# The gates of the latent attention from seven products of quarters

## The chip, the cores and the metric

One core of one Trainium2 chip runs the whole program. The metric is the device time of one execution in microseconds (us).

## The reference

The program is one layer of a diffusion backbone for 128 context tokens and 512 latent tokens, 1024 channels each. The normalised tokens `h` go through one wide input projection into four mixers (a recurrence and three attentions); each mixer's output is projected to 1024 channels, multiplied by a gate per token and channel, and the four are added:

```
h = rmsnorm(x) * (1 + sc1) + sh1
u = h @ w_in                       # among them the gates: 4 x 1024 channels
br[n] = o[n] @ w_branch[n]         # n: recurrence, window, latent, grouped attention
y = sum_n br[n] * sigmoid(gates[n]) @ w_out
```

After that come a norm, an MLP with squared ReLU (1024 to 4096 and back) and a second norm. The change concerns `sigmoid(gates[2])`, the gates of the latent attention: a product of the 1024 x 1024 columns of `w_in` with the 640 tokens.

## The kernel before

All 640 tokens (T) are worked on together. Operands of a product are kept as two parts, hi and lo, whose sum is the fp32 value; a product of a 128 x 128 weight block with 320 tokens (HALF) is three matmuls, hi x hi, hi x lo and lo x hi, added in PSUM (`t_steps`, L357, matmuls at L365 to L367). Weights come as fp32 tiles of 512 KB by DMA on SyncE's queue (`wload`, L311, tag `wr`), and `wsplit` (L322) makes hi by a copy (`copy_r`, L137 and L139, on GpSimd, or ScalarE where `wtile.act` is set, L329) and lo by a subtraction on VectorE (`rest`, L141 and L142). Each of the tags wr, wh and wl has three buffers (WBUFS).

`gates(n)` (L703) calls `gate_steps` (L692): for each of 8 blocks of 128 channels one weight tile, two token halves, for each half 8 blocks of the inner dimension and three matmuls into a bank `mm` (two of them), and a copy out by ScalarE (L698); after four blocks a sigmoid over the four (L701). `merge(n, ...)` (L971) projects a mixer's output in the same form, multiplies by the gates and adds to yT on VectorE (L984, L985).

The latent attention stands in `mla()` (L1037). It first projects the tokens to queries' and keys' latents (`tok_group`, 416 columns, banks of `sc_tile` and one `pv`), then, token tile by token tile (five of 128), squares and scales them (L1075 to L1082), rotates a part, makes `kr4` on GpSimd (L1059) and transposes the pieces on TensorE (L1052, L1061, L1095) into `cq` and `ckv`. Then follow `merge(3, ...)`, `sig = gates(n)`, the loads of w_uq and w_ukv (L1109), the queries' projection and the attention itself, beside which modulation weights (`wada`) go through the same `wr` buffers.

The order of instructions on each engine is fixed when the program is built: a planner takes, for each engine, what is ready by its own estimate of time, work that stands earlier in the program first. Around the change nothing else fixes an order. Buffers are shared by tags: `big` tiles of 2560 elements (14, SLOTS), `small` tiles (tag tk, four), P and PT of the attention units (two each, L760), banks `mm` and `sc` (two each; an sc tile is two banks, of which `sc_bank` uses one).

The MLP already uses the construction that the change brings to the gates: `token_sums` (L1358), `weight_sums` (L1372), `pair` (L1391) with `products` (L1315). There seven products of quarters (4 inner blocks, 320 tokens) stand for two channel blocks and two token halves.

Of the kernel before, what the change touches and what calls it, by code (L numbers as in the profile page):

```python
# [26 lines left out]
OFF = {}  # L27
# [37 lines left out]
def trunk(ctx, tc, I, O):  # L65
# [68 lines left out]
    def f(ap):  # L134
        return ap.bitcast(F32)
# [5 lines left out]
    def rest(out, src, hi):  # L141
        V.tensor_tensor(out=out, in0=src, in1=f(hi), op=ALU.subtract)  # L142
# [168 lines left out]
    def wload(rows, k0, c0, n, nk):  # L311

        raw = wp.tile([128, 1024], F32, tag="wr", name="wr")
        v = lambda t: t[:, 0:nk * n].rearrange("p (k n) -> p k n", k=nk)
        for part, src in rows(k0, nk, c0, n):
            dst = v(raw)[part]
            if len(src.shape) < 3 or len(dst.shape) < 3:
                dst = dst.rearrange("p (a d) -> p a d", d=src.shape[-1])
            dma(out=dst, in_=src)
        return raw  # L320
# [382 lines left out]
    def gates(n):  # L703
        sig = [big(F32, 4, T, name="sig") for _ in range(2)]
        for _ in gate_steps(n, sig):
            pass
        return sig
# [326 lines left out]
    sig3 = gates(3)  # L1034


    def mla():  # L1037
        n = 2
        MS = 96.0 ** -0.5
# [31 lines left out]
        for tt in range(NT):  # L1071
            ps = banks[tt]
            x = small(name="mtx")
            ssq = sm.tile([128, 2], F32, tag="ssq2", name="ssq2")
            S.activation(out=x[:, 0:256], in_=ps[:, 0:256], func=AF.Square, accum_out=ssq[:, 0:1])  # L1075
            S.activation(out=x[:, 256:384], in_=ps[:, 256:384], func=AF.Square, accum_out=ssq[:, 1:2])
            r = sm.tile([128, 2], F32, tag="rs2", name="rs2")
            V.tensor_scalar(out=ssq[:, 1:2], in0=ssq[:, 1:2], scalar1=2.0, scalar2=None, op0=ALU.mult)
            rsqrt_mean(ssq, 2, 256, r)
            V.scalar_tensor_tensor(out=x[:, 0:256], in0=ps[:, 0:256], scalar=r[:, 0:1], in1=qg, op0=ALU.mult, op1=ALU.mult)  # L1080
            V.scalar_tensor_tensor(out=x[:, 256:384], in0=ps[:, 256:384], scalar=r[:, 1:2], in1=kg, op0=ALU.mult, op1=ALU.mult)
            S.activation(out=x[:, 384:416], in_=ps[:, 384:416], func=AF.Copy)  # L1082
            if tt == 4:
                dma(out=O['mla_ckv'], in_=x[:, 256:384])
                dma(out=O['mla_kr'], in_=x[:, 384:416])
                kr = x[:, 384:416]
            else:
                kr = x[:, 416:448]
                rope(x[:, 384:416], 1, 32, tt, rope32, kr)
            key0 = 128 * (tt + 1)  # L1090
            ckv_T(x[:, 256:384], key0)
            kr_T(kr, key0)
            tp = tp_tile()
            for j in range(2):
                PE.transpose(out=tp[:, j], in_=x[:, 128 * j:128 * j + 128], identity=ident)  # L1095
            hi = cq[:, 0, :, 128 * tt:128 * tt + 128]
            S.activation(out=hi, in_=tp[:, 0:2], func=AF.Copy)
            rest(cq[:, 1, :, 128 * tt:128 * tt + 128], tp[:, 0:2], hi)
        merge(3, True, sig3)

        sig = gates(n)

        wu = {}
        for nm, src, nk, a, b in (('uq', I['mla_w_uq'][0], 2, 64, 32), ('ukv', I['mla_w_ukv'][0], 1, 64, 64)):
# [207 lines left out]
    def relu2_tile():  # L1312
        return mx.tile([128, HALF], F32, tag="relu2", name="relu2", bufs=3)

    def products(ps, w, x, start=True, stop=True):  # L1315
        for k in range(len(w)):
            PE.matmul(out=ps, lhsT=w[k][0], rhs=x[k][0], start=(start and k == 0), stop=False)  # L1317
            PE.matmul(out=ps, lhsT=w[k][0], rhs=x[k][1], start=False, stop=False)  # L1318
            PE.matmul(out=ps, lhsT=w[k][1], rhs=x[k][0], start=False, stop=(stop and k == len(w) - 1))  # L1319

    def block(w, m, th, parts=((0, HALF),)):

        ps, sq = mm_tile()[:, 0:HALF], relu2_tile()
# [45 lines left out]
            sums[i] = [(hi[:, k], lo[:, k]) for k in range(4)]  # L1369
        return [by_k(h2[0][0]), by_k(h2[1][0]), by_k(h2[1][1])] + [sums[i] for i in (1, 2, 3, 4)]  # L1370

    def weight_sums(c0):  # L1372

        r1, r2 = (wload(w1, 0, c0 + 128 * m, 128, 8) for m in range(2))
        sa = wp.tile([128, 1024], F32, tag="wr", name="ws")
        p, q = slice(0, 512), slice(512, 1024)

        def split(x, nk):
            hi, lo = wsplit(x, 128, nk)
            return [[(hi[:, k], lo[:, k]) for k in range(i, i + 4)] for i in range(0, nk, 4)]  # L1380
        a11, a12 = split(r1, 8)
        V.tensor_tensor(out=sa[:, q], in0=r2[:, p], in1=r2[:, q], op=ALU.add)
        V.tensor_tensor(out=sa[:, p], in0=sa[:, q], in1=r1[:, p], op=ALU.subtract)
        g2, g1 = split(sa, 8)
        V.tensor_tensor(out=r2[:, p], in0=r1[:, p], in1=r2[:, p], op=ALU.subtract)
        g3, a22 = split(r2, 8)
        V.tensor_tensor(out=r1[:, q], in0=r1[:, q], in1=sa[:, p], op=ALU.subtract)
        g4, = split(r1[:, q], 4)
        return a11, a12, a22, g1, g2, g3, g4

    def pair(c0, X, hid):  # L1391

        b11, b21, b22, t1, t2, t3, t4 = X
        a11, a12, a22, g1, g2, g3, g4 = weight_sums(c0)

        def product(w, x):
            ps = psl.tile([128, 512], F32, tag="pr", name="pr", bufs=5)[:, 0:HALF]
            products(ps, w, x)
            return ps
# [106 lines left out]
```

## Time and profile before

| | us |
|---|---|
| three runs | 1481.51, 1478.18, 1483.23 |
| median | 1481.51 |
| the profiled execution | 1480.22 |
| its span, first to last instruction | 1478.4 |
| TensorE busy | 1408.9 |
| VectorE busy | 908.0 |
| ScalarE busy | 521.6 |
| GpSimd busy | 396.2 |

PE is TensorE's matmul, PEld its weight load, DVE VectorE, ACT ScalarE, POOL GpSimd, SP SyncE (its queue issues the DMAs). Matmuls overlap, so their durations add up to more than they take; their starts tell the pace. Times of day in the trace are us from the start of the span.

### The profile page before, as it was taken

To read this page: it belongs to the slowest core of one execution; us is meant where nothing else is said; L and a number is where in the kernel's file an instruction comes from. 1 tells how busy PE (TensorE), PEld (TensorE's weight loads), DVE (VectorE), ACT (ScalarE), POOL (GpSimd) and SP (SyncE) were. 2 spreads that over 40 slices of the span, in tenths; PEclk is the share of its full clock that TensorE was granted. 3 is DMA by queue.
4 is the path that set the end of the run, shared out by engine and by line. 5 is a ranking of instruction groups with operands and counts; after the bars stand their busy time and mean duration, and the time that the engine had idled before them with its cause. 6 is when DMAs were issued, how large, how long until landed. Compare 5 with 4: busy or idle time off the path is not lost.

```text
span 1478.4 us, 26650 instructions
## 1 busy us (share of the span) xinstructions
PE 1408.9 (95%) x10825; PEld 1282.2 (87%) x10825; DVE 908.0 (61%) x1643; ACT 521.6 (35%) x1189; POOL 396.2 (27%) x430
## 2 busy tenths in 40 slices
PE   6999999999999899999998988998999999999996
PEld 5898998999899898999997677887988988988985
DVE  4347747466742697441824467656857758767865
ACT  4334343332544225442123565314532212321212
POOL 2015425233322445321313344123101001001014
PEclk9999999999999999999999999999999999999998
DMA  9421212122112131112223711232124332222321
GB/s 325 139 85 54 76 48 66 53 61 58 45 44 52 40 80 29 45 36 69 72 71 119 236 57 43 73 104 67 48 80 137 94 115 86 86 58 86 103 69 72
DMA packets 138227, 121.17 MB, mean 82 GB/s; under 512 B 22296, under 2 KB 119412, under 8 KB 138104
## 3 DMA queue, kind: packets, MB, share of 16 engines
q1 hardware_dynamic: 138104, 119.47, 27.4%
q8 instruction: 85, 1.39, 0.4%
q14 instruction: 38, 0.31, 0.1%
HBM read 115.96 MB, written 3.49 MB: 81 GB/s over the span
## 4 chain that ended last, share of the span: by engine, by line
PE 83%; DVE 8%; POOL 3%; ACT 3%; issue 3%; DMA 1%; DVEq 0%; POOLq 0%; ACTq 0%
PE mm L365 8%; PE mm L367 8%; PE mm L366 8%; PE out L381 5%; PE out L383 5%; PE out L382 5%; PE pr L1317 4%; PE pr L1318 4%; PE pr L1319 4%; PE tp L860 3%; PE pv L1013 3%; PE sc L383 3%; PE sc L381 3%; PE sc L382 2%; PE sc L953 2%
## 5 line engine op out<-in xcount | busy, mean ns | idle before, releaser
L142 DVE TENSOR_TENSOR wl<-wr,wh 128x1024 fp32r<-128x1024 f32 (+3 forms) x174 | 209.4, 1207 | 134.9 <-POOL wh L139 81.4
L139 POOL TENSOR_SCALAR wh<-wr 128x1024 fp32r<-128x1024 f32 (+2 forms) x108 | 121.0, 1122 | 549.9 <-PE pr L1319 246.6
L365 PE MATMUL mm<-hTh,wh 128*128 128x320 f32 x704 | 220.4, 313 | 2.0 <-DVE qA L520 0.9
L367 PE MATMUL mm<-hTh,wl 128*128 128x320 f32 x704 | 219.1, 311 | 0.0
L366 PE MATMUL mm<-hTl,wh 128*128 128x320 f32 x704 | 218.1, 310 | 0.0
L365 PEld LDWEIGHTS mm<-hTh,wh 128*128 128x128 f32 x704 | 132.2, 188 | 3.9 <-DVE qA L520 1.0
L813 POOL TENSOR_SCALAR P<-P,rden 128x640 f32<-128x640 f32 (+3 forms) x120 | 84.5, 713 | 183.4 <-DVE rden L825 87.3
L367 PEld LDWEIGHTS mm<-hTh,wl 128*128 128x128 f32 x704 | 132.2, 188 | 0.9 <-issue 0.7
L366 PEld LDWEIGHTS mm<-hTl,wh 128*128 128x128 f32 x704 | 132.2, 188 | 0.5 <-issue 0.3
L383 PE MATMUL out<-wh,hid 128*128 128x512 f32 x320 | 124.8, 390 | 0.0
L382 PE MATMUL out<-wl,hid 128*128 128x512 f32 x320 | 124.6, 389 | 0.0
L381 PE MATMUL out<-wh,hid 128*128 128x512 f32 x320 | 123.5, 391 | 0.0
L329 ACT ACTIVATE wh<-wr 128x1024 fp32r<-128x1024 f32 (+1 forms) x66 | 63.8, 968 | 131.7 <-PE out L383 77.0
L1435 DVE TENSOR_TENSOR y<-out,y 128x512 f32<-128x512 f32 x70 | 47.3, 687 | 52.1 <-PE out L383 52.1
L381 PE MATMUL sc<-wh,hTh 128*128 128x256 f32 (+2 forms) x224 | 71.9, 322 | 5.4 <-ACT hTh L454 2.2
L860 PE MATMUL tp<-ident,P 128*128 128x128 f32 x456 | 72.3, 280 | 3.0 <-DVE modcol L242 1.1
L381 PEld LDWEIGHTS out<-wh,hid 128*128 128x128 f32 x320 | 60.0, 188 | 14.2 <-issue 2.1
L383 PEld LDWEIGHTS out<-wh,hid 128*128 128x128 f32 x320 | 60.0, 188 | 13.4 <-issue 0.8
L598 POOL TENSOR_TENSOR hk<-hk,hf 128x640 f32<-128x640 f32 x28 | 56.6, 2041 | 55.9 <-DVE hf L599 25.0
L383 PE MATMUL sc<-wh,hTl 128*128 128x256 f32 (+2 forms) x224 | 71.0, 317 | 0.3
L382 PEld LDWEIGHTS out<-wl,hid 128*128 128x128 f32 x320 | 60.1, 188 | 12.2
L382 PE MATMUL sc<-wl,hTh 128*128 128x256 f32 (+2 forms) x224 | 70.5, 315 | 0.0
(385 smaller groups left out, 3652.6 us busy)
## 6 DMA issues: line engine op xcount, KB each, us to landing
wr<-in_w_in SPq DMA_DIRECT2D x56, 512.0 KB, 3.7
wada<-in_w_ada SPq DMA_DIRECT2D x48, 512.0 KB, 5.0
wr<-in_w_mlp_in SPq DMA_DIRECT2D x32, 512.0 KB, 4.1
wr<-in_w_mlp_out SPq DMA_DIRECT2D x32, 512.0 KB, 3.8
wr<-in_w_in SPq DMA_DIRECT2D x64, 64.0 KB, 2.1
wr<-in_w_branch SPq DMA_DIRECT2D x8, 512.0 KB, 4.0
wr<-in_w_branch SPq DMA_DIRECT2D x16, 256.0 KB, 4.2
wr<-in_w_out SPq DMA_DIRECT2D x8, 512.0 KB, 3.5
```

The source lines that it names most:

```text
L139: G.tensor_scalar(out=out, in0=src, scalar1=1.0, scalar2=1.0, op0=ALU.mult, op1=ALU.mult)
L142: V.tensor_tensor(out=out, in0=src, in1=f(hi), op=ALU.subtract)
L329: S.activation(out=hi[:, 0:m], in_=raw[:, 0:m], func=AF.Copy)
L365: PE.matmul(out=ps[:, 0:tn], lhsT=wh, rhs=a, start=(k == 0), stop=False)
L366: PE.matmul(out=ps[:, 0:tn], lhsT=wh, rhs=b, start=False, stop=False)
L367: PE.matmul(out=ps[:, 0:tn], lhsT=wl, rhs=a, start=False, stop=(k == nk - 1))
L381: PE.matmul(out=ps[:, 0:n], lhsT=a, rhs=w[k][0], start=(start and k == 0), stop=False)
L382: PE.matmul(out=ps[:, 0:n], lhsT=a, rhs=w[k][1], start=False, stop=False)
L383: PE.matmul(out=ps[:, 0:n], lhsT=b, rhs=w[k][0], start=False, stop=(stop and k == nk - 1))
L813: G.tensor_scalar(out=Pt[:, i, 0:W], in0=Pt[:, i, 0:W], scalar1=rden[:, i:i + 1], scalar2=1.0, op0=ALU.mult, op1=ALU.mult)
L860: PE.transpose(out=tp[:, kk, i], in_=Pt[:, i, 128 * (kt + kk):128 * (kt + kk) + 128], identity=ident)
L1317: PE.matmul(out=ps, lhsT=w[k][0], rhs=x[k][0], start=(start and k == 0), stop=False)
```

## The change

`gates(n)` in `mla()` is replaced by `gates_by_seven(n, X)`, and `X = hT_sums()` is put in front of merge(3). `weight_sums` and `products` move up so that both users find them; `weight_sums` now takes the weight as an argument. The MLP's use of them stays as it was.

```diff
+    def hT_sums():
+
+        def q(kh, th):
+            return [x[:, :, HALF * th:HALF * th + HALF] for x in (h_hi[kh], h_lo[kh])]
+
+        def room(i):
+            tag = ("P", "PT")[i % 2]
+            t = at.tile([128, 2, 640] if tag == "P" else [128, 5, 2, 128], F32, tag=tag, name=tag)
...
+        b = {}
+        for i, (kh, th) in enumerate(((0, 0), (0, 1), (1, 1), (1, 0))):
+            hi, lo = q(kh, th)
+            b[kh, th] = room(i)
+            V.tensor_tensor(out=b[kh, th], in0=f(hi), in1=f(lo), op=ALU.add)
+        b11, b12, b22, b21 = b[0, 0], b[0, 1], b[1, 1], b[1, 0]
+        for out, x, y in ((b11, b12, b11), (b12, b22, b12), (b22, b22, b11), (b21, b21, b22)):
+            V.tensor_tensor(out=out, in0=x, in1=y, op=ALU.subtract)
+        sums = {}
+        for i, src in ((1, b11), (2, b22), (3, b12), (4, b21)):
+            x = big(F32R, 2, 4, HALF, name="hsum")
+            S.activation(out=x[:, 0], in_=src, func=AF.Copy)
+            rest(x[:, 1], src, x[:, 0])
+            sums[i] = [(x[:, 0, k], x[:, 1, k]) for k in range(4)]
...
+    def gates_by_seven(n, X):
+        b11, b21, b22, t1, t2, t3, t4 = X
+        sig = [big(F32, 4, T, name="sig") for _ in range(2)]
+        turn = [0]
+
+        def product(w, x):
+            turn[0] += 1
+            ps = (mm_tile() if turn[0] % 2 else sc_bank())[:, 0:HALF]
+            products(ps, w, x)
+            return ps
+
+        def add(p, q, out=None):
+            out = small(HALF, name="gsum") if out is None else out
+            V.tensor_tensor(out=out, in0=p, in1=q, op=ALU.add)
+            return out
+
+        def keep(ps):
+            x = small(HALF, name="gkeep")
+            S.activation(out=x, in_=ps, func=AF.Copy)
+            return x
+        for p in range(4):
+            c = [[sig[p // 2][:, (2 * p + m) % 4, HALF * th:HALF * th + HALF] for th in range(2)] for m in range(2)]
+            wtile.act = True
+            a11, a12, a22, g1, g2, g3, g4 = weight_sums(w_in, OFF['gates'] + n * 1024 + 256 * p)
+            wtile.act = False
+            p1 = keep(product(a11, b11))
+            add(p1, product(a12, b21), c[0][0])
+            u2 = add(p1, product(g2, t2))
+            p5 = keep(product(g1, t1))
+            u4 = add(u2, p5)
+            u3 = add(u2, product(g3, t3))
+            add(u3, p5, c[1][1])
+            add(u4, product(g4, b22), c[0][1])
+            add(u3, product(a22, t4), c[1][0])
+            if p % 2:
+                S.activation(out=sig[p // 2], in_=sig[p // 2], func=AF.Sigmoid)
+        return sig
...
+        X = hT_sums()
         merge(3, True, sig3)
 
-        sig = gates(n)
+        sig = gates_by_seven(n, X)
```

`weight_sums` as it stands in both versions: two tiles r1, r2 of two channel blocks, a third raw tile for sums, four splits of 8, 8, 8 and 4 inner blocks:

```python
        a11, a12 = split(r1, 8)
        V.tensor_tensor(out=sa[:, q], in0=r2[:, p], in1=r2[:, q], op=ALU.add)
        V.tensor_tensor(out=sa[:, p], in0=sa[:, q], in1=r1[:, p], op=ALU.subtract)
        g2, g1 = split(sa, 8)
        V.tensor_tensor(out=r2[:, p], in0=r1[:, p], in1=r2[:, p], op=ALU.subtract)
        g3, a22 = split(r2, 8)
        V.tensor_tensor(out=r1[:, q], in0=r1[:, q], in1=sa[:, p], op=ALU.subtract)
        g4, = split(r1[:, q], 4)
```

## Rows read from the trace of the kernel before

**Rows 1.** The page: busy time of the engines, and the chain's shares.

```profile
PE 1408.9 (95%) x10825; PEld 1282.2 (87%) x10825; DVE 908.0 (61%) x1643; ACT 521.6 (35%) x1189; POOL 396.2 (27%) x430
PE 83%; DVE 8%; POOL 3%; ACT 3%; issue 3%; DMA 1%; DVEq 0%; POOLq 0%; ACTq 0%
```

**Rows 2.** Busy time by stretch (columns in the first line): projection, merge(3), gates, MLP pairs.

```profile
core 0: us, PE busy (x) PEld busy (x) DVE busy (x) ACT busy (x) POOL busy (x), PEclk, DMA share, GB/s
683.00:702.00 19.00, 19.00 (x104) 18.76 (x103) 3.77 (x5) 4.42 (x6) 3.55 (x3) 1.00 0.35 82
706.00:735.60 29.60, 29.60 (x205) 29.34 (x204) 25.42 (x62) 4.58 (x22) 9.03 (x12) 1.00 0.34 89
735.60:792.70 57.10, 57.10 (x394) 57.06 (x393) 15.15 (x28) 12.07 (x29) 10.92 (x15) 1.00 0.25 72
1157.30:1182.10 24.80, 24.80 (x170) 24.58 (x168) 21.55 (x36) 9.54 (x16) 2.27 (x2) 1.00 0.34 100
```

**Rows 3.** Timeline of PE: start, duration, instruction; borders of gates and MLP pairs.

```profile
735.39 0.31 PE L365 MATMUL mm<-hTh,wh 128*128 128x320 f32 x1
...
792.83 0.28 PE L381 MATMUL mm<-wh,cq 128*128 128x256 f32 x1
...
1157.39 0.30 PE L1317 MATMUL pr<-h2T,wh 128*128 128x320 f32 x1
...
1182.11 0.42 PE L211 MATMUL ada<-wada,cpad 128*32 128x256 f32 x4
```

**Rows 4.** DVE's groups by line and shape from 1000 us on: count, busy, mean ns.

```profile
L142 DVE TENSOR_TENSOR wl<-wr,wh 128x1024 fp32r<-128x1024 f32 x63 | 77.5, 1231 | 29.0 <-ACT wh L329 15.2 <-POOL wh L139 13.8
...
L1406 DVE TENSOR_TENSOR relu<-u,pr 128x320 f32<-128x320 f32 x28 | 13.3, 476 | 0.3 <-PE pr L1319 0.3
...
L1382 DVE TENSOR_TENSOR ws<-wr 128x512 f32<-128x512 f32 x14 | 9.6, 689 | 11.2 <-DMA wr<-in_w_mlp_in 11.2
...
L1362 DVE TENSOR_TENSOR h2f<-h2f 128x1280 f32<-128x1280 f32 x4 | 6.8, 1693 | 1.0 <-ACT h2f L1246 1.0
...
L142 DVE TENSOR_TENSOR tsum<-h2f,tsum 128x1280 fp32r<-128x1280 f32 x4 | 5.9, 1478 | 0.0
```

**Rows 5.** ACT's groups by line and shape from 1000 us on.

```profile
L329 ACT ACTIVATE wh<-wr 128x1024 fp32r<-128x1024 f32 x28 | 29.7, 1060 | 100.6 <-PE out L383 77.0 <-DMA wr<-in_w_mlp_in 11.3 <-PE pr L1318 10.8
...
L1409 ACT ACTIVATE p<-pr 128x320 f32<-128x320 f32 x14 | 6.0, 430 | 5.9 <-PE pr L1319 5.9
```

**Rows 6.** Timeline of DVE beside the projection; in brackets the idle time before.

```profile
694.70 1.03 DVE L142 TENSOR_TENSOR wl<-wr,wh 128x832 fp32r<-128x832 f32 x1 [6.72 <-POOL wh L139]
```

**Rows 7.** Timeline of DVE: keys' scaling of the last two token tiles.

```profile
736.55 0.34 DVE L1081 SCALAR_TENSOR_TENSOR mtx<-sc,rs,mkg 128x128 f32<-128x128 f32 x1
...
748.36 0.34 DVE L1081 SCALAR_TENSOR_TENSOR mtx<-pv,rs,mkg 128x128 f32<-128x128 f32 x1
```

**Rows 8.** Timeline of PE: two of the tokens' transposes among the gates' matmuls.

```profile
737.30 0.38 PE L1095 MATMUL tp<-ident,mtx 128*128 128x128 f32 x2
...
745.54 0.27 PE L1061 MATMUL tp<-ident,kr 128*128 128x128 f32 x1
```

**Rows 9.** Timeline of POOL: kr4 of the token tile before the last.

```profile
739.41 0.29 POOL L1059 COPY kr<-mtx 128x128 f32<-128x128 f32 x1 [0.68 <-DVE mtx L774]
```

**Rows 10.** Busy time and granted clock (PEclk) around a pause of PE.

```profile
276.00:278.00 2.00, 0.55 (x4) 0.55 (x5) 1.63 (x6) 1.08 (x3) 0.00 (x0) 0.99 0.24 49
278.00:280.00 2.00, 2.00 (x12) 2.00 (x11) 0.80 (x3) 0.04 (x1) 0.00 (x0) 0.50 0.84 279
280.00:282.00 2.00, 2.00 (x14) 2.00 (x14) 1.29 (x4) 0.66 (x4) 0.00 (x0) 0.66 0.11 33
```

**Rows 11.** Timeline of SP's queue: the loads of w_uq.

```profile
760.07 7.42 SPq L1109 DMA_DIRECT2D wr<-in_mla_w_uq  x2
```

**Rows 12.** The page's DMA issues: count, KB each, us from issue to landing.

```profile
wr<-in_w_in SPq DMA_DIRECT2D x56, 512.0 KB, 3.7
```

**Rows 13.** Timeline of DVE: an MLP pair's first weight sum and its last whole split.

```profile
1164.07 0.69 DVE L1382 TENSOR_TENSOR ws<-wr 128x512 f32<-128x512 f32 x1 [0.72 <-DMA wr<-in_w_mlp_in]
...
1171.96 1.21 DVE L142 TENSOR_TENSOR wl<-wr,wh 128x1024 fp32r<-128x1024 f32 x1
```

More of the change, by code (lines that the diff above doesn't have):

```diff
@@ L1034, in trunk, with products, weight_sums, split @@
     sig3 = gates(3)
+    def products(ps, w, x, start=True, stop=True):
+        for k in range(len(w)):
+            PE.matmul(out=ps, lhsT=w[k][0], rhs=x[k][0], start=(start and k == 0), stop=False)
+            PE.matmul(out=ps, lhsT=w[k][0], rhs=x[k][1], start=False, stop=False)
+            PE.matmul(out=ps, lhsT=w[k][1], rhs=x[k][0], start=False, stop=(stop and k == len(w) - 1))
+    def weight_sums(rows, c0):
+        r1, r2 = (wload(rows, 0, c0 + 128 * m, 128, 8) for m in range(2))
+        sa = wp.tile([128, 1024], F32, tag="wr", name="ws")
+        p, q = slice(0, 512), slice(512, 1024)
+        def split(x, nk):
+            hi, lo = wsplit(x, 128, nk)
+            return [[(hi[:, k], lo[:, k]) for k in range(i, i + 4)] for i in range(0, nk, 4)]
+        a11, a12 = split(r1, 8)
+        V.tensor_tensor(out=sa[:, q], in0=r2[:, p], in1=r2[:, q], op=ALU.add)
+        V.tensor_tensor(out=sa[:, p], in0=sa[:, q], in1=r1[:, p], op=ALU.subtract)
+        g2, g1 = split(sa, 8)
+        V.tensor_tensor(out=r2[:, p], in0=r1[:, p], in1=r2[:, p], op=ALU.subtract)
+        g3, a22 = split(r2, 8)
+        V.tensor_tensor(out=r1[:, q], in0=r1[:, q], in1=sa[:, p], op=ALU.subtract)
+        g4, = split(r1[:, q], 4)
+        return a11, a12, a22, g1, g2, g3, g4
@@ new lines, in hT_sums @@
+    def hT_sums():
[4 more added lines that the diff above has]
+            t = at.tile([128, 2, 640] if tag == "P" else [128, 5, 2, 128], F32, tag=tag, name=tag)
+            t = t.rearrange("p a b -> p (a b)") if tag == "P" else t.rearrange("p a b c -> p (a b c)")
+            return t.rearrange("p (k t) -> p k t", k=4)
+        b = {}
[12 more added lines that the diff above has]
+            sums[i] = [(x[:, 0, k], x[:, 1, k]) for k in range(4)]
+        whole = []
+        for kh, th in ((0, 0), (1, 0), (1, 1)):
+            hi, lo = q(kh, th)
+            whole.append([(hi[:, k], lo[:, k]) for k in range(4)])
+        return whole + [sums[i] for i in (1, 2, 3, 4)]
@@ L1313, in relu2_tile @@
         return mx.tile([128, HALF], F32, tag="relu2", name="relu2", bufs=3)
[L1315 to L1319, printed above, removed]
     def block(w, m, th, parts=((0, HALF),)):
@@ L1370, in token_sums @@
         return [by_k(h2[0][0]), by_k(h2[1][0]), by_k(h2[1][1])] + [sums[i] for i in (1, 2, 3, 4)]
[L1372 to L1389, printed above, removed]
     def pair(c0, X, hid):
         b11, b21, b22, t1, t2, t3, t4 = X
-        a11, a12, a22, g1, g2, g3, g4 = weight_sums(c0)
+        a11, a12, a22, g1, g2, g3, g4 = weight_sums(w1, c0)
         def product(w, x):
```

## Prediction

> **What bounds the kernel now.** I read the page's busy line and its chain first: PE is busy for 95% of the span and 83% of the chain that ended last is PE work [rows 1], so what counts is how long TensorE needs and whether it stops. Then I read the three stretches that the change touches: the latent branch's input projection, merge(3) and the gates. In all three PE is busy from end to end at the full clock (19.00 of 19.00, 29.60 of 29.60, 57.10 of 57.10 us), while DVE is busy for 3.77, 25.42 and 15.15 us of them [rows 2]. So fewer matmuls in the gates shorten the run directly, as long as PE still never waits there; and DVE has room beside the projection and the gates, but hardly any beside merge(3). As busy time overlaps, I took the pace from starts: the kernel already has the same construction in its MLP, where two pairs run back to back, 168 matmuls of 320 columns from 1157.39 to 1182.11 [rows 3], 24.72 / 168 = 0.147 us each. The gates take from 735.39 to 792.83 [rows 3], 57.4 us: 384 x 0.147 = 56.5, and ten transposes of the token work.
>
> **Part 1, the products.** Before: 8 channel blocks x 2 token halves x 8 x 3 = 384 matmuls. After: 4 pairs x 7 products x 4 x 3 = 336 of the same shape. 48 x 0.147 = **-7.1 us**. Nothing hides this and nothing could give more, since PE has no idle time in the stretch.
>
> **Part 2, the work that pays for it.** By the MLP's rows [rows 4], DVE does per pair 3.5 subtractions that split weights (3 x 1.23 + 0.69 = 4.4 us), 4 sums of weights (4 x 0.69 = 2.8) and 7 additions of products (7 x 0.48 = 3.3): 10.5 us, 42 in all, in place of 8 x 1.23 = 9.8. ACT takes the weight copies over from POOL (about 3.7 us a pair at 1.06 each) and two copies of products (0.43 each) [rows 5]; about 4.6 us a pair against PE's 84 x 0.147 = 12.4, so ACT isn't near its limit, and POOL only loses work.
>
> **Part 3, the token sums ahead of merge(3).** Eight additions and subtractions of 1280 columns and four splits: 8 x 1.69 + 4 x 1.48 = 19.4 us of DVE [rows 4], and four copies on ACT. Their scratch, the P and PT tiles, is free when the attention before ends, and beside the projection DVE is idle for some 15 of 19 us [rows 2], 6.72 of them in one piece [rows 6]. That hides most. Two things don't fit there. Of 14 big slots 12 are held (hT 4, yT 2, the branch's output 2, its gates 2, cq, ckv), so only sums 1 and 2 get a slot; 3 and 4 wait until merge(3) frees some. They feed products 5 and 7 of the first pair, due 7.1 and 10.6 us into the gates; a copy and a split need about 3 us, so that is in time. And the split at 694.70 is needed by PE at once: a sum of 1.5 us ahead of it on DVE can hold PE. Beside merge(3) the first pair's weight sums come on top of 25.4 of 29.6 us; they are last in the program's order there, and most are due only after the merge. Bounds 0 (all hidden) to 3 us (two sums ahead of a needed split); I take **+0.5**, nearer to hidden, since DVE's idle time is so large where the sums are ready.
>
> **Part 4, a new wait at the first pair.** The first product is copied into one of the four small buffers (tk), and these are still in use by the tokens' normalisation: two hold its gains until L1081 of the last token, the other two go round among mtx, rt and kr4. In the trace that last L1081 ends at 748.7, the one of the token before at 736.9 [rows 7]: 13.3 us after the gates' start. Today nothing minds, because the gates use no small buffer. After, PE has four banks (two mm, two sc), four products, 4 x 1.76 = 7.1 us and some transposes, and stops if the first copy still waits then. Behind that copy on ACT stand weight copies of the pair, behind the addition on DVE the next splits. At today's pace the stop is 13.3 + 0.4 - 7.3 = 6.4 us, less the 0.8 us by which transposes run during it: 5.6. But the pace is set by PE's queue: the transposes stand at 737.30 and 745.54, 3.5 to 4.5 us of matmuls apart [rows 8], while the data was ready earlier (kr4 at 739.7 [rows 9]). If they ran when ready, kr4's transpose is at 740, the last token's squares and scaling take the 2.9 us from 745.8 to 748.7, and the stop is about 0.5. Bounds 0 to 5.6; I take **+2.5**, near the middle: the order in the queue stays, but a stopped PE has nothing ahead of the next transpose. Then the clock: where PE stood idle for about 1.5 of 2 us (276 to 278), the granted clock was 0.50 and 0.66 in the next two stretches of 2 us [rows 10], that is 1.2 GHz for about 3.4 us and some 1.7 us lost. A stop of 2.5 us may or may not do that: bounds 0 to 1.7, I take **+0.9**.
>
> **Part 5, pair to pair.** A pair takes all three raw weight buffers, so the next pair's loads wait on SP's queue for its splits, and w_uq's two loads at 760.07 [rows 11] and the modulation's loads behind them wait too. One turn of that ring: a load lands after 3.7 us [rows 12], and from the first weight sum (1164.07, just landed) to the end of the split that frees a buffer (1171.96 + 1.21) the MLP took 9.1 us [rows 13]; 12.8 us, against 12.4 of matmuls. Without the MLP's activation between, DVE is quicker; against that, DVE is fuller: 15.2 - 7.4 (six of the old splits) + 42 - 4 (made ahead) + 3 (late sums) = 49 of some 50 us by the sum of durations. Bounds 0 (the MLP's two pairs didn't stop PE) to 4 us; I take **+1.0**. At the end, w_uq's splits come after the last pair's instead of 10 us ahead of need, and wait for a weight buffer that the sixth product frees 1.8 us before the end: about 2.3 us of POOL and DVE. Bounds 0 to 2, I take **+0.5**. The latent attention behind is the same work in the same order; I take 0.
>
> **The sum.** -7.1 + 0.5 + 2.5 + 0.9 + 1.0 + 0.5 = -1.7. The profiled execution took 1480.22 us (span 1478.4), so 1478.5. The runs' median is 1481.51; against it the forecast is 0.2% lower.
>
> **A rule to weigh.** After a PE pause of about 1.5 us in the trace the clock fell to half once and came back [rows 10]. The Trainium skill, TensorE: Matmul & The Clock Gate, section "A second HAM failure mode: psum-queue depth-cycling", tells of a kernel that cycles through PSUM banks, pauses often between groups of matmuls, and loses its throughput to a clock that goes up and down. By the trace (two MLP pairs cycling five banks, clock 1.00 throughout [rows 2]) it needn't; by the rule it could happen in every pair. It is the third rival.
>
> **The rivals.** *Cover holds everywhere* (faster): the tokens' transposes run as early as their data, stop 0.5, no loss of clock, ring as in the MLP; -7.1 + 0.5 to 3.0, about 1475. For it: the MLP's pairs run at 0.147 with DVE busy for 21.55 of 24.80 us [rows 2]. Against: there other matmuls stand before the pairs, and the first splits are made beside them.
> *The ring paces the pairs* (slower): if an addition that waits for its product stands in DVE's queue ahead of a split, a turn takes 12.8 + 1.8 (a product) = 14.6 us against 12.4. Three turns lose 6.6, and three stops with half the clock's price 2.7; with the other terms 4.4 + 9.3 - 7.1 = +6.6, about 1487. It makes the change a loss of over 0.3% from a turn of about 14.3 us on. For it: four pairs in a row, where the MLP has two and then other matmuls. Against: MLP rows at the limit without a stop.
> *The clock falls in every pair*: 4 x 1.7 in place of 0.9: +5.9 on the forecast, about 1484.
> That the seven products don't come about I exclude; the count of matmuls is plain from the code.
>
> **How the numbers follow.** Chances: forecast (1476.5 to 1481) 0.37, cover holds 0.34, the clock falls in every pair 0.06, ring 0.23. What a measurement of this kernel can tell from no change is about 0.3%, 4.4 us. So faster 0.34, within 0.3% 0.37 + 0.06 = 0.43, slower 0.23. The bounds of the terms give 1473.1 to 1489.5; the forecast's own range is 1476.5 to 1481. The range for 8 in 10 goes from 1472.5, a little under the full gain, to 1487, the ring's centre.
>
> **What would show it.** Matmuls of the gates: 336 at 0.147. Part 3: DVE busy with sums of 1280 columns before merge(3) begins, PE busy throughout the projection. Part 4: PE idle before the fifth product of the first pair, released by ACT's copy, with the last L1081 just ahead, and the clock after it. Part 5: PE idle before the first product of pairs two to four, released by a split, that in turn by a DMA; DVE over 90% busy. The prediction is wrong if PE's starts show no gap in the gates (then about 1474), or if a gap comes back in each pair.

## The result and the profile after

| | kernel before | changed kernel |
|---|---|---|
| median of 12 runs, us | 1480.30 | 1488.99 (1481.04 to 1491.04) |
| ratio, 95% interval | 1 | 1.0054 (1.0043 to 1.0066) |
| profiled execution, us | 1480.22 | 1485.71 |
| its span | 1478.4 | 1483.9 |
| from merge(3)'s first product to w_uq's first, us | 86.90 | 92.49 |
| what comes behind, us | 685.57 | 685.92 |

The change costs half a per cent, some 8 us, where 7.1 us of matmuls went; the median lies 2 us above the range for 8 in 10 (1472.5 to 1487). In the profiled executions the whole difference lies between merge(3)'s first product and the first one that uses w_uq: 92.49 - 86.90 = 5.6 us. I call this part, 87 us long before the change, the stretch; the table of the experiments gives it for each kernel. The lines of the token work have moved: L1052, L1061, L1080, L1081 and L1095 of before are L1147, L1156, L1175, L1176 and L1190 now, the products are L1040 to L1042, the copy of a kept product L1111.

TensorE's timeline of the changed kernel (start, duration; in brackets the idle time before and what ended it), the borders and the places where it stood, to hold against [rows 3] and [rows 8]:

```profile
705.49 0.31 PE L365 MATMUL mm<-oh,wh 128*128 128x320 f32 x1
...
739.51 0.31 PE L1040 MATMUL mm<-hTh,wh 128*128 128x320 f32 x1
...
745.09 0.33 PE L1147 MATMUL tp<-ident,mtx 128*128 128x128 f32 x1
747.77 0.45 PE L1156 MATMUL tp<-ident,kr 128*128 128x128 f32 x1 [2.35 <-DVE ckv L142]
750.24 0.69 PE L1190 MATMUL tp<-ident,mtx 128*128 128x128 f32 x2 [2.02 <-DVE ckv L142]
752.75 0.45 PE L1147 MATMUL tp<-ident,mtx 128*128 128x128 f32 x1 [1.82 <-DVE mtx L1176]
753.21 0.64 PE L1040 MATMUL mm<-hsum,wh 128*128 128x320 f32 x1
...
797.98 0.28 PE L381 MATMUL mm<-wh,cq 128*128 128x256 f32 x1
```

From 745.09 to 753.21 TensorE did five transposes (one line is two of them) and nothing else. The line at 753.21 is the first pair's fifth product. In TensorE's fixed order it stands behind these transposes, so the waits on record are theirs. What it needed itself, the bank of the first product, stands on two other engines: VectorE's timeline has the scaling of the last token's keys,

```profile
752.26 0.34 DVE L1176 SCALAR_TENSOR_TENSOR mtx<-pv,rs,mkg 128x128 f32<-128x128 f32 x1
```

and ScalarE's has, 0.13 us after that one's end, the copy of the first product, which had been ready for 11 us:

```profile
752.73 0.43 ACT L1111 ACTIVATE gkeep<-mm 128x320 f32<-128x320 f32 x1
```

Busy time by stretch around the stop (columns in the first line; PEclk is the granted clock):

```profile
core 0: us, PE busy (x) PEld busy (x) DVE busy (x) ACT busy (x) POOL busy (x), PEclk, DMA share, GB/s
742.00:745.00 3.00, 3.00 (x22) 2.91 (x20) 3.00 (x6) 0.66 (x2) 0.92 (x1) 1.00 0.00 0
745.00:748.00 3.00, 0.65 (x4) 0.32 (x2) 1.80 (x6) 1.22 (x2) 0.29 (x1) 0.94 0.68 178
748.00:751.00 3.00, 0.90 (x3) 0.29 (x2) 2.90 (x7) 0.94 (x6) 0.00 (x0) 0.50 0.00 0
751.00:754.00 3.00, 1.24 (x4) 0.97 (x5) 2.02 (x7) 1.15 (x4) 0.99 (x2) 0.50 0.08 23
754.00:757.00 3.00, 3.00 (x13) 2.96 (x12) 0.28 (x2) 0.44 (x1) 0.00 (x0) 0.50 0.03 4
757.00:760.00 3.00, 3.00 (x20) 3.00 (x19) 1.76 (x5) 1.25 (x3) 0.00 (x0) 0.85 0.00 0
```

The granted clock fell to 0.50, which is 1.2 GHz, while TensorE stood, and stayed there through 754 to 757, when it was busy from end to end again: 13 matmuls in 3 us in place of some 20. The same view of merge(3) and of the other three pairs, to hold against [rows 2]:

```profile
705.40:739.50 34.10, 31.84 (x216) 31.02 (x215) 31.12 (x68) 10.31 (x27) 7.99 (x9) 1.00 0.18 47
...
760.00:797.90 37.90, 37.90 (x261) 37.90 (x260) 28.29 (x46) 14.23 (x18) 2.31 (x4) 1.00 0.38 104
```

In merge(3) TensorE was busy for 31.84 of 34.10 us, with VectorE at 31.12; in the last three pairs it never stopped, the clock was whole, and VectorE had a quarter of the time left. TensorE's waits in the stretch, summed (what waited, for what, us in total, times, longest):

```profile
PE tp L1156 <- DVE ckv L142: 2.4, 1, 2.4
PE tp L1190 <- DVE ckv L142: 2.0, 1, 2.0
PE tp L1147 <- DVE mtx L1176: 1.8, 1, 1.8
PE mm L365 <- DVE sig L984: 1.3, 1, 1.3
PE sc L1040 <- ACT wh L329: 1.0, 1, 1.0
```

The last two are merge(3)'s: a bank that VectorE hadn't emptied, and a weight that ScalarE hadn't rounded for the one product that the planner had put into merge(3) (its twelve matmuls stand among those of the merge).

A transpose costs 0.1 us in a stream of matmuls: the gates of before took 57.4 us for 384 matmuls, 56.5 us, and ten transposes. So the bill of the stretch reads:
- 48 matmuls less: -7.1. Twenty products from 762.78 to 797.98 start 1.76 apart, 12 x 0.147.
- merge(3): 739.51 - 705.49 = 34.0, less 1.76 for the product inside it, is 32.3; before it was 735.39 - 705.93 = 29.5. **+2.8.**
- the stop: 8.1 us for five transposes that cost 0.5 in a stream of matmuls. **+7.6.**
- the clock: products five and six, 24 matmuls and three transposes, took 6.06 us (753.21 to 759.27) where 3.8 would do. **+2.2.**

That is +5.5; the stretch grew by 5.6.

### The profile page after: what moved, and what is told of

Same layout as the page of the kernel before. It is cut to its first block, busy times and chain, and to the rows that moved or that the text cites. A ratio compares the mean times of both kernels' runs of the same rounds, so it can differ in the third digit from the quotient of the medians.

```text
span 1483.9 us, 26646 instructions
## 1 busy us (share of the span) xinstructions
PE 1406.8 (95%) x10777; PEld 1277.3 (86%) x10777; DVE 952.6 (64%) x1707; ACT 537.4 (36%) x1201; POOL 394.4 (27%) x422
## 5 line engine op out<-in xcount | busy, mean ns | idle before, releaser
L139 POOL TENSOR_SCALAR wh<-wr 128x1024 fp32r<-128x1024 f32 (+2 forms) x100 | 116.2, 1163 | 545.4 <-PE pr L1042 247.6
L365 PE MATMUL mm<-hTh,wh 128*128 128x320 f32 x576 | 180.8, 314 | 2.0 <-DVE qA L520 0.9
L367 PE MATMUL mm<-hTh,wl 128*128 128x320 f32 x576 | 179.4, 312 | 0.0
L366 PE MATMUL mm<-hTl,wh 128*128 128x320 f32 x576 | 178.2, 309 | 0.0
L329 ACT ACTIVATE wh<-wr 128x1024 fp32r<-128x1024 f32 (+1 forms) x78 | 74.8, 960 | 148.0 <-PE out L383 77.3
L365 PEld LDWEIGHTS mm<-hTh,wh 128*128 128x128 f32 x576 | 108.2, 188 | 3.9 <-DVE qA L520 1.0
L367 PEld LDWEIGHTS mm<-hTh,wl 128*128 128x128 f32 x576 | 108.2, 188 | 1.0 <-issue 0.9
L366 PEld LDWEIGHTS mm<-hTl,wh 128*128 128x128 f32 x576 | 108.2, 188 | 0.3 <-issue 0.2
```

Source lines behind the costliest of these rows:

```text
L139: G.tensor_scalar(out=out, in0=src, scalar1=1.0, scalar2=1.0, op0=ALU.mult, op1=ALU.mult)
L329: S.activation(out=hi[:, 0:m], in_=raw[:, 0:m], func=AF.Copy)
L365: PE.matmul(out=ps[:, 0:tn], lhsT=wh, rhs=a, start=(k == 0), stop=False)
L366: PE.matmul(out=ps[:, 0:tn], lhsT=wh, rhs=b, start=False, stop=False)
L367: PE.matmul(out=ps[:, 0:tn], lhsT=wl, rhs=a, start=False, stop=(k == nk - 1))
```

## The experiments

Three theories. **A**: the first pair needs a small buffer that the last token holds; without that wait the gain comes out. **B**: VectorE has too much to do beside merge(3), whoever waits. **C**, later: the first pair's weight roundings hold up the tokens' copies on ScalarE. A fourth, D, came out of a run that went the wrong way. All kernels in one table ("sums early": the token sums are asked for ahead of the token steps; "by eight": the first pair is made by eight products as before the change); "last scaling" is the end of the last L1176 (or its counterpart) less the start of the matmul that follows merge(3)'s last one.

| kernel | ratio to before (95%) | median, us | stretch, us | last scaling, us |
|---|---|---|---|---|
| before | 1 | 1479.07 to 1480.30 | 86.90 | 13.3 |
| changed | 1.0054 (1.0043 to 1.0066) | 1488.99 | 92.49 | 13.1 |
| changed, again | 1.0050 (1.0036 to 1.0065) | 1487.69 | 92.58 | 13.2 |
| token sums alone | 1.0027 (1.0015 to 1.0039) | 1484.06 | 91.37 | 13.3 |
| seven products alone | 1.0033 (1.0021 to 1.0046) | 1484.96 | 90.06 | 13.6 |
| gains in own tile | 1.0009 (0.9995 to 1.0023) | 1481.80 | 86.20 | 1.3 |
| before, gains in own tile | 0.9998 (0.9983 to 1.0012) | 1478.74 | 86.82 | 1.5 |
| first pair's roundings on GpSimd | 1.0058 (1.0039 to 1.0076) | 1487.55 | 94.33 | 13.9 |
| the same, gains in own tile | 1.0028 (1.0015 to 1.0042) | 1483.18 | 88.26 | 1.3 |
| splits on GpSimd, gains in own tile | 1.0052 (1.0036 to 1.0069) | 1487.81 | 92.41 | 0.9 |
| sums early | 1.0103 (1.0082 to 1.0124) | 1494.30 | 99.51 | 23.4 |
| sums early, gains in own tile | 1.0051 (1.0036 to 1.0065) | 1487.77 | 92.09 | 13.5 |
| sums early, queries' buffer held | 1.0024 (1.0010 to 1.0038) | 1484.33 | 89.47 | 12.9 |
| the same, gains in own tile | 0.9981 (0.9969 to 0.9993) | 1478.34 | 81.77 | -0.4 |
| first pair by eight | 0.9982 (0.9973 to 0.9990) | 1476.86 | 83.80 | 16.0 |
| the same, again | 0.9981 (0.9968 to 0.9993) | 1478.47 | 83.75 | 15.9 |
| first pair by eight, gains in own tile | 1.0001 (0.9990 to 1.0012) | 1479.47 | 84.07 | 3.5 |
| first pair by eight, sums early, buffer held | 0.9969 (0.9953 to 0.9985) | 1474.99 | 81.70 | 15.9 |

In the five kernels with early sums, four of merge(3)'s matmuls (0.6 us) stand ahead of it, in the projection, and the stretch is counted from where merge(3) goes on: against the other kernels 0.6 us has to be added to it.

What comes behind the stretch took 683.8 to 690.9 us in these profiles, without a pattern that I could tie to an edit. So the medians tell which kernel is faster, and the stretch tells where the time went. The two don't quite agree: in the fifteen rows with seven products the median, against the kernel before, is worse than the stretch says by up to 3.2 us (2.2 on the mean; one lies at 0), and in the two others with eight products throughout they agree to 0.3 us. What the seven products cost outside the stretch isn't found.

### The changed kernel again

> The changed kernel once more, for a second profile and as the base of the others. Theory A (the wait): the first pair's fifth product waits again some 6 us for the keep copy behind the last token's scaling, the granted clock falls to about 0.5 for some 9 us behind it; ratio to the kernel before 1.004 to 1.007. Theory B (VectorE is the limit beside merge(3)): the same ratio. This run tells nothing between them; it tells how far stop, clock and span move from profile to profile (the first changed profile was 1485.7, its median 1489.0), and what the other kernels of this call are set against.

The stop came back with the same three waits (2.4, 2.2 and 1.8 us), and the stretch to 0.1 us. What differed from the first profile lay behind: 687.8 us in place of 685.9.

### One half at a time: the sums alone, the seven products alone

```diff
-        sig = gates_by_seven(n, X)
+        sig = gates(n)
```

> The token sums and their splits are made as in the changed kernel, but nothing reads them: the gates are the kernel before's, with eight products' worth of matmuls. Theory A: the sums alone put VectorE back by at most their four splits (5.9 us), of which merge(3) shows 2.3 us of stops; gates of the old form don't wait for a small buffer behind the tokens, so the kernel before plus 1 to 3 us, 1481 to 1483.5. Theory B: the splits beside merge(3) are the price whatever the gates are; the kernel before plus 6 us or more, 1486 or more.

The sums alone cost 0.27%, and all of it is in merge(3): 737.49 - 703.53 = 34.0 us in place of 29.5, +4.5, of which 3.3 are waits for L984 on record; the gates behind took 57.4 us as before. VectorE's timeline inside merge(3) shows how:

```profile
719.72 2.32 DVE L142 TENSOR_TENSOR hsum<-PT,hsum 128x1280 fp32r<-128x1280 f32 x1
721.96 0.48 DVE L985 TENSOR_TENSOR yT<-yT,sig 128x320 f32<-128x320 f32 x1
722.37 0.48 DVE L984 TENSOR_TENSOR sig<-mm,sig 128x320 f32<-128x320 f32 x1
722.77 1.47 DVE L142 TENSOR_TENSOR hsum<-PT,hsum 128x1280 fp32r<-128x1280 f32 x1
724.17 1.21 DVE L142 TENSOR_TENSOR wl<-wr,wh 128x1024 fp32r<-128x1024 f32 x1
725.30 0.48 DVE L984 TENSOR_TENSOR sig<-mm,sig 128x320 f32<-128x320 f32 x1
```

and TensorE's, in the same 6 us:

```profile
722.90 0.42 PE L365 MATMUL mm<-oh,wh 128*128 128x320 f32 x1 [1.52 <-DVE sig L984]
...
725.83 0.41 PE L365 MATMUL mm<-oh,wh 128*128 128x320 f32 x1 [0.91 <-DVE sig L984]
```

An eviction (L984) frees one of two banks; a product fills a bank in 1.76 us. With a 1.5 to 2.3 us split in front of it the eviction is late and TensorE stops. That is neither as small as A had it nor as large as B.

In the other half the four sums are left out:

```diff
-        return whole + [sums[i] for i in (1, 2, 3, 4)]
+        return whole + [whole[i] for i in (0, 1, 2, 0)]
```

> The seven products take whole quarters in place of the four token sums, which are left out with their adds, subtractions, copies and splits (so the gates are other numbers); all matmuls, weight sums, waits for small buffers and additions stay. Theory A: the wait for the last token's buffer stays, but the last token ends up to 5.9 us earlier, since four splits (1.48 us each) are gone from VectorE: stop 0 to 4 us in place of 6.2; 1476 to 1482. Theory B: with VectorE free of the splits nothing is left of the loss: the kernel before less the 48 matmuls' 7.1 us, 1473 to 1475, and no stop at the fifth product.

Both were wrong. Merge(3) was whole again (31.3 us, less 1.76 for the product in it, is 29.5), but the stop stayed: TensorE's waits in the stretch,

```profile
PE tp L1142 <- DVE ckv L142: 4.4, 1, 4.4
PE tp L1133 <- DVE mtx L1162: 1.7, 1, 1.7
...
PE tp L1176 <- DVE ckv L142: 0.7, 1, 0.7
```

and the stretch is 90.06 = 86.90 - 7.06 + 10.2. The stop with its clock is 10.2 us without a single token sum in VectorE's queue, where the changed kernel had 7.6 + 2.2. The last token's scaling ended 13.6 us after merge(3), against 13.1 in the changed kernel and 13.3 in the kernel before. So the token sums don't set it. The first pair's weight sums, which this kernel keeps, have a share: behind the transpose that precedes the longest wait, ScalarE's copy was done at 747.2, but VectorE, whose order is fixed too, did three weight sums and a split of weights first,

```profile
746.98 0.26 ACT L1135 ACTIVATE ckv<-tp 128x128 fp32r<-128x128 f32 x1
...
747.13 0.69 DVE L1054 TENSOR_TENSOR ws<-wr 128x512 f32<-128x512 f32 x1 [3.04 <-DMA wr<-in_w_in]
...
749.07 1.22 DVE L142 TENSOR_TENSOR wl<-wr,wh 128x1024 fp32r<-128x1024 f32 x1
750.20 0.28 DVE L142 TENSOR_TENSOR ckv<-tp,ckv 128x128 fp32r<-128x128 f32 x1
```

the first of which had waited for its weights from DMA.

### The gains out of the small buffers

```diff
-        qg = small(256, name="mqg")
-        kg = small(128, name="mkg")
+        qg, kg = gains[:, 0:256], gains[:, 256:384]
```

(`gains` is a tile of 128 x 384 in the mixers' pool, shared with the two gains of the grouped attention, which is over by then.)

> The changed kernel with the two rows of norm gains of the latent projections in a tile of their own, so that they no longer hold two of the four small buffers that tokens and gates share. VectorE's and ScalarE's work are unchanged. Theory A (the first pair's keep copy waits for a small buffer that the last token holds; stop 6.2 us and some 2 us of clock): the fifth product no longer waits for the last token, stop and clock loss go, about 8 us less than the changed kernel, 1480 to 1482. Theory B (VectorE has too much work beside merge(3), whoever waits): with the buffer there, the first pair's sums still stand behind the same work of VectorE, PE fills the four banks and stops elsewhere; 1486 to 1489 as the changed kernel.

Inside A's range (1480 to 1482): 5.9 us less than the changed kernel on the same chip, where A had said about 8. The last token's scaling now ends 1.3 us after merge(3) in place of 13: two more buffers go round among the tokens, so that several tokens can be under way where it was one at a time. VectorE has the same work as in the changed kernel, so B in the form "whoever waits" is out. The clock stayed at 1.00 through the stretch. What is left are short waits:

```profile
PE mm L1040 <- DVE gsum L1106: 1.7, 1, 1.7
PE sc L1040 <- ACT wh L329: 1.0, 1, 1.0
PE mm L365 <- DVE sig L984: 1.0, 1, 1.0
PE tp L1155 <- DVE cq L142: 0.8, 1, 0.8
PE mm L1040 <- ACT gkeep L1111: 0.7, 1, 0.7
```

The control has the same edit in the kernel before.

> Control: the kernel before, with eight products, and the two gains in a tile of their own. Theory A: the gates of before wait for no small buffer, so nothing is gained: within 1.5 us of the kernel before, 1478 to 1481.5. Rival: two more small buffers also free the token steps or the attention behind, and the gain seen in the changed kernel is in part one that the kernel before would have had too: 1474 to 1477.

There too the tokens end 12 us earlier (1.5 us after merge(3)), and the time is the same to 0.1%: with eight products nobody waits for them. The slow tokens cost nothing until the first pair made something wait behind them. The edit's worth was much the same wherever seven products come first: 6.3 us of the stretch here, 6.1 with the roundings moved, 7.4 and 7.7 with early sums.

### Weight roundings on GpSimd

```diff
-            wtile.act = True
+            wtile.act = p > 0
```

> The changed kernel with only that edit: the first pair's roundings on GpSimd, the gains left where they were. Theory A: the keep behind the last token stays the wait that ends last; the tokens before it may run up to 2 us sooner: 1485 to 1489. Theory C: the tokens are late because of the roundings, and with them gone from ScalarE the stop shrinks by half or more: 1481 to 1485.

> The gains in a tile of their own, and the first pair's weight roundings (four) run on GpSimd in place of ScalarE, where they stood in front of the tokens' copies; PE's order is unchanged against the kernel with the gains alone (ratio 1.0009). Theory C (roundings that wait for a weight buffer hold up the tokens' copies behind them on ScalarE): the stops of the first pair (0.8 + 0.7 + 1.7 us) shrink, and that of merge(3) for a rounding (1.0 us): 1477 to 1480. Theory B (VectorE): nothing, since VectorE's work is the same, 1480.5 to 1483.

C isn't borne out. The medians missed its ranges (1487.55 against 1481 to 1485, 1483.18 against 1477 to 1480). The stops stayed where they were, and the stretch was 1.8 and 2.1 us longer than without the edit. The roundings have a price on GpSimd, too: the product inside merge(3) now waited 1.5 us for GpSimd's rounding in place of 1.0 for ScalarE's.

### The splits on GpSimd

```diff
-            rest(x[:, 1], src, x[:, 0])
+            G.tensor_tensor(out=x[:, 1], in0=src, in1=f(x[:, 0]), op=ALU.subtract)
```

> As the kernel with the gains in a tile of their own, and the four splits of the token sums run on GpSimd in place of VectorE (same order asked for). VectorE loses 5.9 us of work beside merge(3); no row shows a subtraction of 1280 columns on GpSimd, whose largest, the 1024-column rounding, takes 1.04 us. Theory A: merge(3)'s stops (1.0 + 1.0 us) and most of the first pair's go: 1477 to 1480. Rival: GpSimd's splits are slow or disturb VectorE's, products that read them come late, and the stops change their place: 1481 to 1485.

The rival in kind, and beyond its range (1487.81 against 1481 to 1485). A split took 2.9 to 3.3 us on GpSimd, and VectorE got slower beside it; the last section has the rows. Merge(3)'s stops grew from 2.0 to 4.5 us, and what the own tile for the gains had brought was gone.

### The sums asked for earlier

```diff
         banks = tok_group(w_in, OFF['mcq'], 416, hT, fifth=pv_tile)
+        X = hT_sums()
...
-        X = hT_sums()
         merge(3, True, sig3)
```

> As the kernel with the gains in a tile of their own (ratio 1.0009), and the token sums are asked for ahead of the latent projection's token steps in place of behind them, so that the planner puts three of the four copies and splits into the idle time of ScalarE and VectorE beside the projection. Theory A (two separate costs: the small buffer's wait, some 6 us, already gone; and late splits beside merge(3)): the stops in merge(3) (1.0 + 1.0 us) go and those of the first pair (0.8 + 0.7 + 1.7 us) shrink, 3 to 5 us less than that kernel, 1477 to 1479, faster than the kernel before. Theory B (VectorE is full beside merge(3) with the weight sums and tokens alone): the place of the splits matters little; within 1.5 us of 1481.

> The changed kernel with the token sums asked for ahead of the token steps, the gains left where they were: the fourth corner of two edits. Theory A: the stop at the fifth product comes from the small buffer and the last token's chain, and stays (6 to 7 us as where the sums were left out, plus the clock's 2); only merge(3)'s stops of 2.3 us go: 1485 to 1487. Theory B: with the splits out of the way the tokens end earlier and the stop shrinks with them by 4 us or more: 1481 to 1483.

Neither theory had it: 6 and 7 us slower than without the edit, where A had a gain and B no change in the one and a gain in the other. With the gains in their own tile merge(3) ran without a stop, since three splits started at 690, 695 and 696 us; but the tokens came to a halt. TensorE wrote the first token's latent queries for transposing at

```profile
716.96 0.38 PE L1190 MATMUL tp<-ident,mtx 128*128 128x128 f32 x2
```

and ScalarE's copy of them, with everything behind it on ScalarE, ran 22 us later, as soon as merge(3)'s last product was through (on TensorE at 738.54):

```profile
738.75 0.39 ACT L1192 ACTIVATE cq<-tp 128x256 fp32r<-128x256 f32 x1 [5.98 <-PE mm L366]
```

The copy's target `cq` is one of the 14 big buffers. In the kernel before its first write came ahead of any sum; now three sums came first, and the suspicion (D) was that they took what was free, so that cq had to wait for one that merge(3) still read. The next edit gives cq its buffer first and changes nothing else:

```diff
+        S.activation(out=cq[:, 0, 0, 0:1], in_=eye32[:, 0:1], func=AF.Copy)
         X = hT_sums()
```

> The same without moving the gains: token sums early, the queries' buffer held first. Theory A with D: the small buffers' wait at the fifth product (6 us and the clock's 2) remains, merge(3)'s stops go: 1484 to 1487, against 1494 for early sums without the held buffer. Theory B: no better than that, 1490 or more.

> Gains in a tile of their own, token sums asked for ahead of the token steps, and one column of the latent queries' tile is written before them, so that it gets its big buffer first. Theory D (the early sums made the kernel slower only because they took the queries' buffer, so that their first copy, and all of ScalarE behind it, waited 6.0 us for merge(3)'s last product): the token steps go on through merge(3), two of four splits lie ahead of it; merge(3)'s stops (2.0 us) go and the first pair's shrink against the kernel with the gains alone: 1476 to 1480. Theory B (VectorE and the weight sums): as early sums without the held buffer, 1485 to 1489.

D holds: the stretch fell by 10.0 us (99.51 to 89.47) and by 10.3 (92.09 to 81.77). Two splits now lie ahead of merge(3) (690.3 and 694.7), the third and fourth later, and the tokens keep their pace. With both causes out of the way the seven products bring most of what they were meant to: 81.77 and the 0.6 us ahead of it are 4.5 us less than before, of 7.1, and the kernel is faster than the one before by 0.2%. With the gains still in the small buffers the stop is back (6.3 us of waits) and merge(3) is whole.

### The first pair by eight products

```diff
+            if p == 0:
+                for m in range(2):
+                    t_block(wgroup(w_in, OFF['gates'] + n * 1024 + 128 * m, 128), 0, hT,
+                            lambda ps, t0, tn, m=m: S.activation(out=sig[0][:, m, t0:t0 + tn], in_=ps, func=AF.Copy))
+                continue
```

> As the kernel with only the first pair in the old form, but with the gains left in the small buffers. Theory A: the three pairs of seven come behind the last token, so the keep of the first of them (14 products later) finds a buffer: the gains' place matters at most 1.5 us, 1475 to 1479. Rival: the keep still waits for the last token, whose steps run slower with two buffers, and the stop only moves some 18 us later: 1480 to 1485.

> Only the first pair of the gates goes back to eight products (24 matmuls per quarter pair, no keeps, no sums), the other three pairs take seven; the gains are in a tile of their own. 36 of the 48 matmuls stay saved (5.3 us). Theory A (the loss is the first pair's meeting with the last tokens: its keep and sums want small buffers, its weight sums stand among the tokens' steps): PE finds plain matmuls between the token steps, as in the kernel before; no stop in the first pair, merge(3)'s stops of 2 us at most remain: 1475 to 1478, faster than the kernel before. Theory B (the sums of tokens and weights beside merge(3) are the price, whichever pair comes first): the splits stay and the loss with them, 1481 to 1484.

> The kernel with only the first pair by eight products once more, for the comparison on the same chip and for a second interval (first: 0.9982, 0.9973 to 0.9990). If its gain is real: 0.997 to 0.999 again; if it came from its one set of runs: 0.999 to 1.001.

The kernel with the gains in the small buffers came out in A's range, and in the second series at the same ratio; the one with the gains in a tile of their own, at 1479.47, missed A's range (1475 to 1478) and B's as well. As A had it, the stop is gone whether the gains are in the small buffers or not: the first two blocks are plain matmuls among which the tokens' transposes stand, and the first kept product comes when the last token is through (its copy ran at 755.0, the last scaling had ended at 753.7). The stretch was 83.8 us; the products alone would be 86.9 - 36 x 0.147 = 81.6. Two series of runs gave 0.998. Where the gains lie made no difference to the stretch (84.07); that this kernel's runs were 0.2% slower isn't explained by it and stays open.

> First pair by eight products, three pairs by seven, and the token sums early with the queries' buffer held first. The stretch from merge(3) to the latent projection took 83.8 us with the sums late, 2.2 more than the products alone (86.9 less 36 times 0.147 is 81.6), of which 1.0 were stops in merge(3). Theory D: those 2.2 us go to 1 or less: 1475 to 1476.5. Rival: two of the four splits lie in merge(3) still and keep the stops: 1476.5 to 1478.

D's forecast. Busy time by stretch, merge(3) and the gates:

```profile
704.10:733.70 29.60, 29.45 (x200) 28.67 (x199) 27.30 (x62) 5.86 (x23) 9.19 (x11) 1.00 0.28 71
733.70:785.80 52.10, 52.10 (x360) 52.06 (x359) 36.14 (x68) 21.59 (x37) 6.05 (x9) 1.00 0.29 78
```

No wait of TensorE is on record in either; the stretch is 81.70, or 82.3 with the 0.6 us ahead of it, 0.7 above the products' 81.6. By its median this is the fastest kernel of the study: 1474.99 us, 0.31% less than the kernel before, though it keeps only 36 of the 48 saved matmuls. Its interval overlaps those of the kernels at 0.998.

## Why the prediction was wrong

**The mechanism was named, its size was not.** The stop stands where Part 4 put it: TensorE idle before the fifth product of the first pair, with the last token's scaling and ScalarE's copy just ahead, and the clock after it. The forecast took 2.5 + 0.9 us; it was 7.6 + 2.2.

**The step that failed** is in Part 4: "If they ran when ready", with the value taken "near the middle", because "a stopped PE has nothing ahead of the next transpose". I let a stopped TensorE speed the tokens up by several us. It didn't: the last scaling ended 13.1 us after merge(3), where [rows 7] had 13.3 with TensorE busy. Each token step goes from TensorE over other engines and back; in the stop three such steps took 2.7, 2.5 and 2.5 us (to 747.77, 750.24 and 752.75), one token after the other, because only two small buffers went round. The run that gave them four shows it: 1.3 us. The row gave the upper end. The argument for the lower one took a transpose to be ready with its data: kr4 was ready at 745.63 here, and its transpose (L1156) stood until 747.77, for VectorE's subtraction on the transpose before it. The steps were that long because a stopped TensorE leaves the other engines' queues as they are, and there the first pair's weight work stood in front, VectorE's splits and weight sums and a rounding on ScalarE:

```profile
745.11 1.06 ACT L329 ACTIVATE wh<-wr 128x1024 fp32r<-128x1024 f32 x1 [2.45 <-issue]
746.07 0.26 ACT L1149 ACTIVATE ckv<-tp 128x128 fp32r<-128x128 f32 x1
746.20 1.23 DVE L142 TENSOR_TENSOR wl<-wr,wh 128x1024 fp32r<-128x1024 f32 x1 [0.99 <-ACT wh L329]
747.34 0.28 DVE L142 TENSOR_TENSOR ckv<-tp,ckv 128x128 fp32r<-128x128 f32 x1
...
748.25 0.28 ACT L1157 ACTIVATE ckv<-tp 128x128 fp32r<-128x128 f32 x1 [1.92 <-PE tp L1156]
749.17 0.68 DVE L1057 TENSOR_TENSOR wr<-wr 128x512 f32<-128x512 f32 x1
749.88 0.29 DVE L142 TENSOR_TENSOR ckv<-tp,ckv 64x128 fp32r<-64x128 f32 x1
```

The first subtraction started 1.0 us after its copy had ended and the second 1.35, the copy of the first 0.65 after its transpose, and the last token's scaling, too, came behind weight sums on VectorE. So it was luck that the last scaling ended as late as before: there the tokens' transposes stood among matmuls [rows 8], here the tokens stood behind weight work. No run takes the weight sums out of VectorE's way, so what they alone cost isn't shown.

**Its upper bound was too low as well**, 5.6 against 7.6. I had counted four products, 7.1 us, as cover behind merge(3). The planner put one of them into merge(3), so the cover was three, and the transposes that ran in the stop, a saving of 0.8 us in the bound, were worth 0.5.

**Part 3** was mis-sized: 0.5 taken, 3 the bound, 2.8 measured in the changed kernel and 4.5 with the sums alone. The eight sums ran from 674 to 691, three ahead of the projection and five beside it, and TensorE ran through it without a stop. But I expected sums 1 and 2 to be split there, too, and all four splits landed at 718, 721, 728 and 741, in merge(3) and just behind. I had looked at what VectorE had free beside the projection and not at the copies ahead of the splits: ScalarE ran the first two at 715.2, behind the first token's copy to cq (714.9), though it had stood idle for nine microseconds before the tokens' squares (701.5). In merge(3), with 25.4 of 29.6 us taken [rows 2], a split of 1.5 us in front of an eviction is a stop, because two banks cover only 1.76 us. The count of the big buffers in that part was right, and the early sums showed what it means when someone takes one more.

**Part 1** was right: 336 matmuls at 0.147. **Part 5** and the end: taken at 1.0 and 0.5, they cost nothing. From the second pair on VectorE was busy for 28.29 of 37.90 us, where Part 5 had 49 of some 50, and no wait is on record, so the ring rival is refuted; so is "cover holds everywhere". Four pairs went through two mm and two sc banks in turn, and once the stop was over the granted clock was 1.00 throughout. What the Trainium skill (TensorE: Matmul & The Clock Gate, section "A second HAM failure mode: psum-queue depth-cycling") tells of didn't happen here.

With the ends of the bounds that the rows carried (5.6, 1.7 and 3) and nothing for the ring and the end, the sum would have been -7.1 + 10.3 = +3.2, a kernel that is slower by 0.2%; with the terms as measured it is +5.5, and the profiled execution was 5.5 us longer. The median of the changed kernel's runs lies another 3.3 us above its profiled execution. Where these 3.3 us lie isn't shown, as the other runs have no trace; the slower of its runs had the lower mean granted clock (0.988 at 1481.04 us, 0.981 at 1491.04), and what lowered it stays open.

## What to carry to other kernels

Before work is put behind a chain of small steps, ask what holds the chain back: a constant that lives in a rotating buffer takes that buffer away from everyone who rotates, and it costs nothing until the next user has to wait for the same set. When a stop is bounded between a row and an argument, take the row: an idle TensorE doesn't speed up work that goes over other engines, whose queues still hold other work ahead of it. And when such a chain can't be shortened, leave plain matmuls beside it and start the clever form one step later; here that gave back more than it cost.

## What the runs showed of the hardware

GpSimd's subtractions stopped VectorE's. In the kernel with the splits on GpSimd, two of them run back to back, 6.43 us in all:

```profile
715.06 6.43 POOL L1085 TENSOR_TENSOR hsum<-P,hsum 128x1280 fp32r<-128x1280 f32 x2 [1.72 <-ACT hsum L1084]
```

VectorE's timeline beside them:

```profile
715.82 2.88 DVE L985 TENSOR_TENSOR yT<-yT,sig 128x320 f32<-128x320 f32 x1
718.62 0.48 DVE L984 TENSOR_TENSOR sig<-mm,sig 128x320 f32<-128x320 f32 x1
719.02 3.02 DVE L1055 TENSOR_TENSOR ws<-ws,wr 128x512 f32<-128x512 f32 x1
```

In the changed kernel L985 takes 0.48 us and L1055 0.68 (medians); here each ended 0.4 to 0.6 us behind one of GpSimd's subtractions (718.34 and 721.49). L984, which reads one operand from PSUM, took its 0.48 in between. The Trainium skill (SBUF — State Buffer, section "SBUF: two separate sides") says that VectorE with two operands in SBUF and GpSimd share one pair of ports, and that whoever comes first keeps it for the whole instruction; these rows agree.

A stop of TensorE cost more than its length: after 8.1 us with five transposes the granted clock stayed at 0.50 for 3 us of full work, and the half clock cost another 2.2 us. In the kernel without token sums it was 8.7 us with five transposes, and another 2.0 us.
